# A two-layer attention backbone on one core: 622 further random shifts in the order of all queues

## The chip, the core and the metric

The kernel runs on one core of a Trainium2 chip. Its engines are TensorE (PE, matrix products), ScalarE (ACT), VectorE (DVE), GpSimd (POOL) and SyncE (SP, which here issues most of the DMAs). The metric is the time of one execution on the device in microseconds (us); several executions are run, and their median is given.

## What is computed

Two layers work on 512 latent tokens and 256 context tokens of width 1024. Each layer normalises and scales its input with factors that come from a conditioning vector, projects it, attends, gates, projects again, normalises and adds. Layer 0 uses differential attention (8 heads, each with two query and key halves of 64), layer 1 grouped-query attention (8 query heads, 2 key and value heads of 128, with normalised queries and keys). Cut to what matters:

```python
for i in range(2):
    shift, scale, gate = split3(silu(c) @ ada_w[i] + ada_b[i])     # and the same from c_ctx for the context
    h  = rms_norm(x, pre_g[i]) * (1 + scale) + shift
    q, k, v, z = split(h @ w_in[i])                                # context tokens alike
    q, k = rope(q), rope(k)                                        # latent tokens only
    if i == 0:                                                     # differential attention
        o = softmax(q1 k1^T / 8) v - lam * softmax(q2 k2^T / 8) v
        o = rms_norm(o, subln_g) * (1 - lam_init)
    else:                                                          # grouped-query attention
        o = softmax(rms(q) rms(k)^T / sqrt(128)) v
    x = x + gate * rms_norm((o * silu(z)) @ w_out[i], post_g[i])   # layer 0: the context stream too
```

Latent queries see latent and context keys in one softmax, context queries see only context keys.

## The kernel before

**Precision.** Every large product is made of three matmuls on operands split in a high and a low part (`mm3`): high by high, high by low, low by high. So each weight tile `raw` that a DMA brings is cast by ACT to `whi`, and POOL or DVE subtracts to get `wlo`; the activations `h` are split the same way, and so are the transposed softmax weights `at` (`ah` by ACT, `al` by DVE, in `split_at`).

**Stages.** First the conditioning factors of layer 0: groups of eight PE matmuls with 32 columns of output rows (`ag` tiles times `s`), ACT copies the result to `row`, PE spreads it with `sel`, DVE makes `mods`. In the same stretch PE transposes the normalised input (`xt` to PSUM, DVE and ACT copy it to `xnt`), and ACT scales it to `h`. Then layer 0: projections of query, key, value and gate, filled in between the attention of one head after the other. The attention of a head and block: PE makes scores into a double PSUM bank (`sc0`, `sc1`), DVE takes the maxima (`sm`), ACT the exponentials `pp` and `p`, DVE combines the two softmaxes in one product (`pp<-p,sm,pp`, SCALAR_TENSOR_TENSOR), transposes within 32 by 32 blocks (STREAM_TRANSPOSE), and SP moves the result to DRAM and back (`dr<-pp`, `at<-dr`) to complete the transposition; then the split, and PE multiplies by the values. Between heads, PE works through twelve groups of conditioning weights of 1 MB for what comes later (`grp_mm`, tile `araw`, one buffer, `grp_load`); ACT or DVE adds the result up in `arow`, DVE transposes it, PE folds it (`fold`), and DVE multiplies out the blocks that are wanted (`fo`, in `folded`). `sq<-bk,eps` is the logarithm by which ACT begins the normalisation of an attention output, out of the PSUM bank in which PE has made the sums of squares (`colsum`). Then the output projection of layer 0, `h` of layer 1 (`hf`, `h`), normalised keys (`kn`, scale `qrs`), and attention of layer 1 in the same way. PSUM has four single banks `bk0` to `bk3` and the two double ones, so that a group of matmuls often has to wait for the engine that empties its bank.

**What sets the order.** The program is run twice. First `Plan` records every instruction with what it reads and writes, works out who depends on whom, and prices each (`price`). Its list scheduler (`schedule`) then plays the program against these prices, picking on each engine the instruction that is ready first and, among those, the one with the lowest key. Twelve such passes (`PASSES`) give a key for each instruction. Then the tuple `MOVES` (line 102) is gone through: for each number in it, `shift` draws a random change of some keys, and a last play with the changed keys gives the order. The second run, `Emit`, issues the instructions, and `chain` ties each to the one before it on its engine, so that the order of the plan is the order on the chip. All instructions of the kernel therefore have one line in the profile, that of `Emit.add` (L526), and are told apart by their tiles.

```python
for s in MOVES:
    self.shift(random.Random(s), key, groups, side)
return self.schedule(lambda o: (key[o], o.n))
```

In `shift`, half of the numbers move a run of 1, 3, 8 or 20 PE groups (a group is all the matmuls into one PSUM output) by up to 30, 80, 200 or 500 in the key, together or each for itself; the other half move 1 to 40 neighbouring instructions of DVE, ACT, POOL or SP by up to 500, 1500 or 4000.

Of the kernel before, what the change touches and what calls it, by code (L numbers as in the profile page):

```python
# [94 lines left out]
def f32(ap):  # L95
# [40 lines left out]
    94403095, 584977676, 619944211, 22435410, 703825272, 621311326, 1059365364, 402415890, 143690719, 745221345,  # L136
    887241769, 694410056, 952138463, 289139968, 159032642, 434187675, 960054692, 918848355, 776950033, 866070713,
    362704586, 896208923, 1025137297, 255630178, 908876465, 71426820, 392273835, 223495391, 1023233858, 475503153,
    364577799, 282150972, 809075548, 442212720, 329900567, 892875344)
SLACK = 0  # L140


# [2255 lines left out]
```

## Time and profile before

| what | us |
|---|---|
| median of 3 runs | 742.43 |
| lowest and highest run | 741.39, 743.15 |
| the profiled execution | 742.12 |
| its span in the trace | 740.3 |
| PE busy | 724.4 |
| DVE, ACT, POOL busy | 545.5, 480.1, 458.6 |

The span runs from the first to the last instruction of the trace; 1.8 us of the profiled execution lie around it. A row of the timeline gives start and length in us, engine, line, operation, the tile written and the tiles read, shapes, and how many like instructions the row takes together; in brackets stands how long the engine was idle before it and what released it. A matmul's length in such a row includes its way through the array; the next one starts before it ends, so the pace of PE is read from start to start. PEld is the loading of weights into PE, which runs beside the matmuls.

### The profile page before, as it was taken

What the parts mean: (1) busy time and instruction counts of PE and PEld (TensorE: products, weight loads), DVE (VectorE), ACT (ScalarE), POOL (GpSimd) and SP (SyncE); (2) the same over time, 40 slices, a digit from 0 to 9 for tenths busy, and PEclk for the clock granted to TensorE, in tenths of its full rate; (3) what the DMA queues carried; (4) which work ended last, traced back from release to release, by engine and by line L of the source; (5) the groups of instructions that cost most, each with busy time, mean ns of one, the idle gap of its engine ahead of it and who ended that gap; (6) DMA issues with size and microseconds to landing.
All of it is one profiled execution on the core that took longest, in us unless ns stands there. A gap on an engine that the chain in (4) does not pass through costs nothing.

```text
span 740.3 us, 13930 instructions
## 1 busy us (share of the span) xinstructions
PE 724.4 (98%) x5008; PEld 648.5 (88%) x5008; DVE 545.5 (74%) x891; ACT 480.1 (65%) x1085; POOL 458.6 (62%) x506
## 2 busy tenths in 40 slices
PE   7999999999999999999999999999999999999996
PEld 6688888898888889888898998899999999988986
DVE  5555788769959876777798853699656789898844
ACT  6635467776577574766578943696366679679641
POOL 5363776785688775785855312447789959855201
PEclk9999999999999999999999999999999999999999
DMA  9941456454557575565557062453447678697613
GB/s 350 406 164 58 143 160 181 147 181 136 179 185 241 187 214 157 170 200 178 175 174 256 16 256 86 143 179 95 134 141 210 191 250 245 203 282 207 179 57 114
DMA packets 52596, 133.85 MB, mean 181 GB/s; under 512 B 6576, under 2 KB 27952, under 8 KB 50992
## 3 DMA queue, kind: packets, MB, share of 16 engines
q1 hardware_dynamic: 49104, 127.95, 54.1%
q10 hardware_dynamic: 3424, 5.02, 2.0%
q8 instruction: 39, 0.64, 0.4%
q14 instruction: 29, 0.24, 0.1%
HBM read 98.61 MB, written 30.15 MB: 174 GB/s over the span
## 4 chain that ended last, share of the span: by engine, by line
PE 68%; DVE 3%; POOL 2%; ACT 1%; issue 1%; DMA 1%; DVEq 0%; ACTq 0%
PE bk L526 56%; PE sc L526 11%; DMA araw<-in_ada_g 1%; POOL wlo L526 1%; POOL q L526 1%; DVE h L526 1%; DVE pp L526 1%; DVE hf L526 0%; ACT hf L526 0%; DVE sm L526 0%; POOL pp L526 0%; POOL qrs L526 0%; DVE sw L526 0%; ACT jk L526 0%; DVE gacc L526 0%
## 5 line engine op out<-in xcount | busy, mean ns | idle before, releaser
L526 PE MATMUL bk<-whi,h 128*128 128x256 f32 (+1 forms) x1184 | 247.3, 299 | 4.2 <-ACT sq L526 1.4
L526 PE MATMUL bk<-h,whi 128*128 128x512 f32 (+2 forms) x832 | 222.8, 348 | 0.0
L526 PEld LDWEIGHTS bk<-whi,h 128*128 128x128 f32 x1184 | 190.9, 188 | 14.8 <-ACT h L526 2.8
L526 POOL TENSOR_TENSOR wlo<-raw,whi 128x256 fp32r<-128x256 f32 x200 | 172.1, 885 | 46.2 <-ACT whi L526 45.7
L526 PE MATMUL bk<-wlo,h 128*128 128x256 f32 (+1 forms) x592 | 174.3, 297 | 0.0
L526 PEld LDWEIGHTS bk<-h,whi 128*128 128x128 f32 x832 | 145.2, 188 | 16.1 <-issue 3.4
L526 PE MATMUL bk<-h,wlo 128*128 128x512 f32 (+2 forms) x416 | 142.7, 348 | 0.0
L526 DVE TENSOR_REDUCE sm<-sc 128x1 f32<-128x768 f32 (+1 forms) x128 | 102.0, 814 | 23.8 <-PE sc L526 16.0
L526 PEld LDWEIGHTS bk<-wlo,h 128*128 128x128 f32 x592 | 110.9, 188 | 3.7
L526 POOL TENSOR_SCALAR pp<-pp,sm 128x768 f32<-128x768 f32 (+1 forms) x78 | 75.8, 976 | 51.0 <-DVE sm L526 34.8
L526 DVE TENSOR_TENSOR al<-at,ah 128x512 fp32r<-128x512 f32 x103 | 88.6, 877 | 16.5 <-ACT ah L526 11.8
L526 PEld LDWEIGHTS bk<-h,wlo 128*128 128x128 f32 x416 | 77.9, 188 | 6.5
L526 ACT CAST whi<-raw 128x1024 fp32r<-128x1024 f32 (+1 forms) x70 | 71.5, 1023 | 17.1 <-PE bk L526 10.9
L526 ACT CAST ah<-at 128x512 fp32r<-128x512 f32 x103 | 61.7, 620 | 14.6 <-PE bk L526 11.5
L526 DVE STREAM_TRANSPOSE pp<-pp 128x1536 f32<-128x1536 f32 (+1 forms) x39 | 61.4, 1575 | 3.0 <-POOL pp L526 2.9
L526 POOL TENSOR_TENSOR sz<-sz,za 128x384 f32<-128x384 f32 (+1 forms) x24 | 28.1, 1172 | 43.6 <-ACT za L526 43.6
L526 PEld LDWEIGHTS sc<-qk,qk 64*128 64x128 f32 x480 | 37.2, 185 | 15.3 <-ACT za L526 3.2
L526 ACT ACTIVATE jk<-bk 128x128 f32<-128x128 f32 (+4 forms) x66 | 22.8, 345 | 40.5 <-PE bk L526 21.3
L526 PE MATMUL sc<-qk,qk 64*128 64x256 f32 (+1 forms) x480 | 48.4, 337 | 0.0
L526 ACT ACTIVATE pp<-sc,sm 128x768 f32<-128x768 f32 (+1 forms) x46 | 35.5, 772 | 19.5 <-DVE sm L526 19.3
L526 DVE SCALAR_TENSOR_TENSOR pp<-p,sm,pp 128x768 f32<-128x768 f32 x32 | 43.8, 1368 | 3.7 <-POOL pp L526 2.9
L526 ACT ACTIVATE za<-za 128x384 f32<-128x384 f32 (+1 forms) x72 | 40.1, 562 | 7.6 <-DVE za L526 7.0
(218 smaller groups left out, 1356.2 us busy)
## 6 DMA issues: line engine op xcount, KB each, us to landing
dr<-pp SPq DMA_DIRECT2D x32, 768.0 KB, 4.0
at<-dr SPq DMA_DIRECT2D x128, 192.0 KB, 4.3
raw<-in_a_w SPq DMA_DIRECT2D x30, 512.0 KB, 4.2
araw<-in_ada_g SPq DMA_DIRECT2D x12, 1024.0 KB, 5.7
raw<-in_b_w SPq DMA_DIRECT2D x20, 512.0 KB, 3.6
ag<-in_ada_s SPq DMA_DIRECT2D x16, 512.0 KB, 9.0
raw<-in_w_out SPq DMA_DIRECT2D x16, 512.0 KB, 4.8
sw<-qr ACTq DMA_DIRECT2D x32, 128.0 KB, 3.2
```

The lines of the kernel that those rows point to most:

```text
L526: self.ops.append(getattr(eng, meth)(*args, **kw))
```

## The change

Only the tuple `MOVES` grows: it had 376 numbers, and 622 more are put behind the last, on 62 further lines. The first line that differs:

```diff
-    364577799, 282150972, 809075548, 442212720, 329900567, 892875344)
+    364577799, 282150972, 809075548, 442212720, 329900567, 892875344, 312439870, 458344974, 449572097, 562893025,
...
+    795406408, 794988788, 385261862, 383781077, 76324529)
```

The numbers were picked for orders that do well in plays of the program in which the landings of DMAs vary and some ACT, DVE and POOL instructions are lengthened at random. The planner, its prices, its passes and the program are the same, and so are the instructions and where their tiles lie: 4892 matmuls, 903 rows of ACT, 891 of DVE, 509 of POOL and 341 of SP in both. In the order, 3211 of the matmuls stand at another place (by up to 103 places), 391 rows of ACT (by up to 11), 372 of DVE (by up to 32), 211 of POOL and 126 of SP (by up to 4). The first 27 or so matmuls and PE's last 45 rows stay. The line of `Emit.add` is L588 after the change.

The prediction speaks of three places above all. In the rows below, a tile's name has its number and its place in the program behind it, and `x4` means four like rows in a run.

*The start, PE.* `ag` are the groups for the factors of layer 0, `xt_12` is a tile of input being transposed, `h_38` the first scaled input and `row_37`, `row_41` are copies of the groups' results. Before:

```order
L526 MATMUL sc1_75<-ident_76,xt_12_167 128x128
L526 MATMUL bk2_72<-sel4_138,row_37_276 128x2
L526 MATMUL sc1_75<-ident_76,xt_12_167 128x128
L526 MATMUL bk1_71<-ag_16_176,s32_134 32x256 x4
L526 MATMUL bk0_70<-whi_5_157,h_38_290 128x256
L526 MATMUL bk0_70<-wlo_6_158,h_38_290 128x256
L526 MATMUL sc0_74<-h_38_290,whi_1_153 128x512
```

After:

```order
L588 MATMUL sc1_75<-ident_76,xt_12_167 128x128 x8
L588 MATMUL bk0_70<-ag_14_171,s32_134 32x256 x4
L588 MATMUL bk1_71<-ag_16_176,s32_134 32x256 x4
L588 MATMUL bk2_72<-sel4_138,row_37_276 128x2 x2
L588 MATMUL bk1_71<-ag_17_178,s32_134 32x256 x4
L588 MATMUL bk0_70<-whi_5_157,h_38_290 128x256
L588 MATMUL bk0_70<-wlo_6_158,h_38_290 128x256
L588 MATMUL bk3_73<-sel4_138,row_41_302 128x2
```

`ag_14`, which stood ahead of all eight transposes of `xt_12`, now stands behind them; `ag_17`, which came twelve rows behind the first `h_38`, now stands ahead of it.

*ACT at the time of 174 us.* `pp_275` and `p_281` are the exponentials of one block of scores, `sq_233` is the logarithm that frees bank `bk0`. Before:

```order
L526 ACTIVATE pp_275_1973,sm_279_2062<-sc0_74,sm_282_2089 128x24x32
L526 ACTIVATE p_281_2088,sm_279_2062<-sc1_75,sm_283_2097 128x768
L526 ACTIVATE sq_233_1697<-bk0_70,eps_85 128x384
L526 ACTIVATE pp_273_1971,sm_279_2062<-sc0_74,sm_282_2089 128x8x32
L526 ACTIVATE at_274_1972,sm_279_2062<-sc1_75,sm_283_2097 128x256
L526 CAST vhi_270_1947<-bk1_71 128x256
```

After:

```order
L588 ACTIVATE pp_275_1973,sm_279_2062<-sc0_74,sm_282_2089 128x24x32
L588 ACTIVATE sq_233_1697<-bk0_70,eps_85 128x384
L588 ACTIVATE p_281_2088,sm_279_2062<-sc1_75,sm_283_2097 128x768
L588 ACTIVATE pp_273_1971,sm_279_2062<-sc0_74,sm_282_2089 128x8x32
L588 CAST vhi_270_1947<-bk1_71 128x256
L588 ACTIVATE at_274_1972,sm_279_2062<-sc1_75,sm_283_2097 128x256
```

`sq_233` has moved ahead of the second exponential.

*DVE at the time of 364 us.* `fo_591` empties bank `bk1` of a folded row, `pp_564` is a softmax block, `gT_470` an attention output, `al` are low parts of `at`. Before:

```order
L526 SCALAR_TENSOR_TENSOR gT_470_3525<-gT_470_3525,subg_112,sq_528_3911 128x768
L526 RECIPROCAL sm_572_4235<-sm_572_4235 128x2
L526 SCALAR_TENSOR_TENSOR za_584_4303<-sz_571_4210,za_584_4303 128x384
L526 TENSOR_SCALAR sm_572_4235<-sm_572_4235,nlam_122 128x2
L526 TENSOR_TENSOR vlo_590_4353<-bk2_72,vhi_589_4352 128x256
L526 TENSOR_TENSOR al_601_4538<-at_554_4097,ah_600_4537 128x512
L526 TENSOR_TENSOR fo_591_4368<-bk1_71,quad_149 128x32
L526 SCALAR_TENSOR_TENSOR pp_564_4172<-p_574_4261,sm_572_4235,pp_564_4172 128x24x32
```

After:

```order
L588 TENSOR_TENSOR al_601_4538<-at_554_4097,ah_600_4537 128x512
L588 TENSOR_SCALAR sm_572_4235<-sm_572_4235,nlam_122 128x2
L588 TENSOR_TENSOR al_603_4551<-at_554_4097,ah_602_4550 128x512
L588 TENSOR_TENSOR vlo_590_4353<-bk3_73,vhi_589_4352 128x256
L588 SCALAR_TENSOR_TENSOR za_584_4303<-sz_571_4210,za_584_4303 128x384
L588 SCALAR_TENSOR_TENSOR pp_564_4172<-p_574_4261,sm_572_4235,pp_564_4172 128x24x32
L588 TENSOR_TENSOR vlo_590_4353<-bk2_72,vhi_589_4352 128x256
L588 STREAM_TRANSPOSE pp_564_4172<-pp_564_4172 128x1536
L588 TENSOR_TENSOR fo_591_4368<-bk1_71,quad_149 128x32
```

`fo_591` has moved behind the product, the transpose, a further `al` and a further `vlo`; `gT_470`, which stood ahead of it, now comes two rows behind it.

61 rows, old and new, of the table MOVES are left out of this document.

## The prediction

> **What bounds the kernel now.** I read the page first, then TensorE's waits, then the timeline around each of those waits. The page's share of busy time:
>
> ```profile
> PE 724.4 (98%) x5008; PEld 648.5 (88%) x5008; DVE 545.5 (74%) x891; ACT 480.1 (65%) x1085; POOL 458.6 (62%) x506
> ```
>
> TensorE (PE) is busy for 98% of the span; the next engine, VectorE (DVE), for 74%. The change alters only orders, and the matmuls stay the same, so a gain can come only out of the time that PE stands still. The view of PE's waits lists all of that (total us, times, longest):
>
> ```profile
> PE bk L526 <- ACT sq L526: 1.4, 1, 1.4
> PE sc L526 <- DVE xt L526: 1.4, 1, 1.4
> PE bk L526 <- ACT h L526: 1.4, 2, 1.1
> PE sc L526 <- POOL xt L526: 1.3, 1, 1.3
> PE bk L526 <- DVE ones L526: 1.0, 1, 1.0
> PE bk L526 <- DMA araw<-in_ada_g: 0.8, 1, 0.8
> PE bk L526 <- DVE fo L526: 0.7, 1, 0.7
> PE bk L526 <- DVE kn L526: 0.6, 1, 0.6
> PE bk L526 <- ACT row L526: 0.5, 1, 0.5
> PE sc L526 <- DVE sm L526: 0.2, 1, 0.2
> PE bk L526 <- DVE h L526: 0.2, 1, 0.2
> ```
>
> They add to 9.5 us. The 1.0 behind `ones` is the first instruction of all and stays. So 8.5 us is the ceiling of any gain, 1.1% of the kernel; there is no such ceiling on a loss, since each of 4892 matmuls can begin to wait. PE's last 45 rows of the order are the same before and after, so the end of the kernel stays as it is. What PE pays for going from one kind of matmul to another I hold equal too: there are 34 runs of 64-row score matmuls in both orders, and 20 against 19 runs of 32-column ones.
>
> **The change part by part.** I followed each wait through the new order of its engines. The price of a matmul is needed throughout; PE's rows at one of the waits give it (start and length in us, then the operation, and in brackets the wait):
>
> ```profile
> 364.37 0.39 PE L526 MATMUL bk<-whi,h 128*128 128x256 f32 x1 [0.65 <-DVE fo L526]
> 364.59 0.28 PE L526 MATMUL bk<-wlo,h 128*128 128x256 f32 x1
> 364.71 0.40 PE L526 MATMUL bk<-whi,h 128*128 128x256 f32 x2
> ```
>
> With its inputs there, a matmul of 256 columns is followed by the next after 364.71 - 364.59 = 0.12, and so I put one of 384 columns at 0.18 (an estimate from the same two rows).
>
> *The start, to 25 us.* PE's rows around the first `h`, the scaled input of the projections:
>
> ```profile
> 15.32 0.85 PE L526 MATMUL sc<-ident,xt 128*128 128x128 f32 x6 [1.41 <-DVE xt L526]
> ...
> 18.44 0.38 PE L526 MATMUL bk<-whi,h 128*128 128x256 f32 x1 [1.13 <-ACT h L526]
> ...
> 20.75 0.64 PE L526 MATMUL bk<-ag,s 128*32 128x256 f32 x8
> 21.93 0.38 PE L526 MATMUL bk<-sel,row 128*128 128x2 f32 x2 [0.55 <-ACT row L526]
> ```
>
> Before, the group `ag_14` (eight matmuls of 256 columns, 0.64 like the row at 20.75) stands ahead of `xt_12` and runs while DVE still works on that; what is left of the wait is 1.41. After, it stands behind, and the transposes of `xt_12` can't start sooner than 15.32, since DVE is no sooner done. (Its load moves back by one place on SP, behind a weight tile's; that is hidden, as nobody asks for it before then.) So 0.64 moves out of idle time onto the path, and the first `h` reaches PE at about 18.44 + 0.6 = 19.05. Against that, `ag_17` (the row at 20.75) now stands ahead of that `h`, inside its 1.13 of idle time, and its `row` is copied long before PE asks for it, so that the 0.55 at 21.93 goes. From `h` to `ag_17` PE worked 20.75 - 18.44 = 2.31; the same work now ends at 19.05 + 2.31 = 21.36, and what stood behind the row at 21.93 goes on from there: 21.93 - 21.36, 0.6 sooner. Term: -0.6. Bounds: -1.2 (the 0.64 and the 0.55 both gained, if `h` isn't late) and +0.7 (the 0.64 lost, and a new wait for the second `h` in place of the rest).
>
> *`sq` at 174.* ACT's and PE's row. Behind them stand three that the next parts need: one softmax product `pp` on DVE with two POOL products running beside it, and one like it without:
>
> ```profile
> 172.58 0.89 ACT L526 ACTIVATE p<-sc,sm 128x768 f32<-128x768 f32 x1
> ```
> ```profile
> 174.09 0.39 PE L526 MATMUL bk<-whi,h 128*128 128x256 f32 x1 [1.41 <-ACT sq L526]
> ```
> ```profile
> 168.45 2.34 DVE L526 SCALAR_TENSOR_TENSOR pp<-p,sm,pp 128x768 f32<-128x768 f32 x1
> ```
> ```profile
> 222.78 1.01 DVE L526 SCALAR_TENSOR_TENSOR pp<-p,sm,pp 128x768 f32<-128x768 f32 x1
> ```
> ```profile
> 168.13 4.36 POOL L526 TENSOR_TENSOR qk<-qr,qk 128x768 fp32r<-128x768 f32 x2
> ```
>
> The logarithm `sq` reads PSUM bank bk0, and PE's next group wants that bank. It moves ahead of one exponential of 0.89, so the bank is free 0.89 sooner. Four matmuls fewer stand in front, which were 4 x 0.12 = 0.5 of cover. Term: 0.89 - 0.5, so -0.4; bounds 0 and -1.1 (with whatever ACT saves ahead of it).
>
> *`araw` at 263.5.* The load of one 1 MB weight tile, its wait, and a row of score matmuls for the price of one:
>
> ```profile
> 254.67 8.79 DMA araw<-in_ada_g
> ```
> ```profile
> 254.54 1.67 PE L526 MATMUL sc<-qk,qk 64*128 64x512 f32 x18
> ...
> 263.51 1.06 PE L526 MATMUL bk<-araw,s 128*32 128x512 f32 x8 [0.78 <-DMA araw<-in_ada_g]
> ```
>
> The tile has one buffer: its load starts when the group before has read it and must land before the next group. Between the two groups stood 27 matmuls of 384 columns and 13 of 256; now there are 34 and 15. That is 7 x 0.18 + 2 x 0.12 = 1.5 more cover, against 0.78 of waiting. Term: -0.8; bounds -0.8 and, if the load takes its longest under other traffic by the same 1.5, 0.
>
> *`fo` at 364.* DVE must take a folded row out of bank bk1 before PE's next group uses the bank; the wait, 0.65, is in the first of the three rows above. DVE's rows:
>
> ```profile
> 359.46 1.42 DVE L526 SCALAR_TENSOR_TENSOR gT<-gT,subg,sq 128x768 f32<-128x768 f32 x1
> ...
> 363.49 0.72 DVE L526 TENSOR_TENSOR al<-at,ah 128x512 fp32r<-128x512 f32 x1
> 364.14 0.18 DVE L526 TENSOR_TENSOR fo<-bk,quad 128x32 f32<-128x32 f32 x1
> 364.24 2.59 DVE L526 SCALAR_TENSOR_TENSOR pp<-p,sm,pp 128x768 f32<-128x768 f32 x1
> 366.76 0.41 DVE L526 TENSOR_TENSOR vlo<-bk,vhi 128x256 fp32r<-128x256 f32 x1
> 367.09 1.76 DVE L526 STREAM_TRANSPOSE pp<-pp 128x1536 f32<-128x1536 f32 x1
> ```
>
> On DVE, `fo` now comes behind the `pp` product, a `vlo`, the transpose and one more `al`, and ahead of `gT`: 2.59 + 0.41 + 1.76 + 0.72 - 1.42 = 4.06 later. On PE, 24 more matmuls of 256 columns and two fewer of 384 stand ahead of the fold (24 x 0.12 - 2 x 0.18 = 2.5), and between the fold and the waiting group there are 7 more of 384 and 12 score matmuls (7 x 0.18 + 12 x 1.67 / 18 = 2.4): 4.9 later in all. 4.06 less 4.9 takes 0.8 off a wait of 0.65: in time by 0.2, too little to be sure of. I take -0.5. Bounds: -0.65; and +0.9, if DVE is held up here by one more collision like that of the 2.34 row, against the lone 1.01 (1.33 late, less the 0.2 to spare, less some 0.2 that the other terms may leave PE behind).
>
> [...]
>
> *`kn` and `h` near 500.* Waits of 0.6 and 0.2 in the list above. DVE's rows up to `kn`, which empties a bank for PE:
>
> ```profile
> 498.27 0.75 DVE L526 SCALAR_TENSOR_TENSOR gacc<-gw,scol,gacc 128x512 f32<-128x512 f32 x1
> 498.94 0.69 DVE L526 TENSOR_TENSOR h<-hf,h 128x512 fp32r<-128x512 f32 x1
> 499.54 0.60 DVE L526 SCALAR_TENSOR_TENSOR kn<-bk,qrs,gq 128x128 f32<-128x128 f32 x2
> ```
>
> Two such subtractions `h` and two `gacc` steps now stand behind `kn` on DVE: up to 2 x 0.69 + 2 x 0.75 = 2.9 sooner. On PE, 12 matmuls of 256 columns and four short transposes (at no more than 0.12) ahead of the waiting group are gone: 16 x 0.12 = 1.9 sooner. That leaves 1.0 against 0.6, if `kn`'s other input, a scale from ACT, comes as early. I take -0.4, with bounds of -0.6 and +0.4 (`kn` won no more than 1.5). For `h`, one of two halves of the step before it now stands behind it: -0.2, bounds -0.2 and 0.
>
> *All the rest.* 3211 matmuls change place, by up to 103 places, and 126 of SP's 341 rows, by up to 4; no other wait is there to be removed. What I could not follow can only add waits. The six terms make -0.6 - 0.4 - 0.8 - 0.5 - 0.4 - 0.2 = -2.9; I give back a quarter of this, 0.7, for new small ones: the list above holds four waits of 0.2 to 0.6, so two such. Sum: -2.2 on the profiled execution (742.12 with a span of 740.3, so 1.8 around it, unchanged). The median of the runs is 742.43, 0.3 above the profiled one; from the median, 742.4 - 2.2 = 740.2.
>
> **The rivals.** 0.2% is 1.5 us, about what a measurement can tell from no change: faster is below 740.95, slower above 743.9.
>
> *Nothing moves.* The waits re-form elsewhere. For it: the terms of `fo` and `kn` win by putting other work of DVE behind (`gT`, two `h`, two `gacc`), and `h` is itself a line in the list of waits. Against it: that list holds nothing of `gT` or `gacc`, so these had some room. If the give-back is the whole 2.9 instead of 0.7: 742.4.
>
> *Slower, by collisions.* The product `pp` starts a chain: transpose, round trip through DRAM, split, matmul. A collision costs 2.34 - 1.01 = 1.33 us on it. If the new order makes four more that PE has no lead left to hide, 4 x 1.33 = 5.3 against the 2.9 won: 742.4 + 2.4 = 744.8. It decides from the third on (4.0 - 2.9 = +1.1), and slower as I call it from the fourth. For it: 32 of these products run, and nothing in an order keeps them off POOL's. Against it: before, the collisions at 168 and 364 cost PE nothing that its list of waits shows under `pp` or `at`.
>
> **How the numbers follow.** The forecast case has 0.60; its own range is 742.4 - 4.5 = 737.9 (every term at its better bound, with nothing given back) to 741.0. Nothing moves: 0.22, between 741.0 and 743.9. Slower: 0.18, of which 0.14 for the collisions and 0.04 for the upper bounds of the start and `fo` coming together (+0.7 + 0.9 with the other terms at naught). The range for 8 in 10 leaves out a tail of the forecast case below 737.8 and most of the slower case: 737.8 to 744.0. Likeliest: 740.2.
>
> **What would show it.** In PE's waits after: no `araw`, no or a smaller `fo`, `kn` and `row`, `sq` at 1.0 or less, and the first `h` about 0.6 later but the second earlier; the sum of waits at about 7.3. I am wrong if the sum of PE's waits is as before or higher, if waits for `at`, `ah` or `al` appear that were not there, or if the waits fall and the span does not, which would say that matmuls themselves issue more slowly in the new order.

## The result and the profile after

Six executions of each kernel, in turns on one chip: 738.1 us after (737.15 to 739.76) against 742.14 before (741.39 to 743.15), 4.0 us less; the ratio is 0.9948, with a 95% interval of 0.9934 to 0.9961. The forecast was 740.2, between 737.8 and 744.0. So the direction and the range held, the latter by 0.3, and the gain was almost twice the forecast. The profiled execution took 738.26, with a span of 736.5 against 740.3.

The page's share of busy time, and the whole list of PE's waits, of the changed kernel:

```profile
PE 723.0 (98%) x5008; PEld 647.4 (88%) x5008; DVE 555.1 (75%) x891; ACT 478.0 (65%) x1085; POOL 460.7 (63%) x506
```
```profile
PE sc L588 <- POOL xt L588: 2.7, 1, 2.7
PE sc L588 <- DVE xt L588: 1.6, 1, 1.6
PE bk L588 <- DVE ones L588: 1.0, 1, 1.0
PE bk L588 <- ACT h L588: 0.9, 2, 0.7
PE bk L588 <- POOL q L588: 0.4, 1, 0.4
PE sc L588 <- DVE sm L588: 0.2, 1, 0.2
```

The waits add to 6.8 instead of 9.5. Gone are `sq`, `araw`, `fo`, `kn`, `row` and the `h` near 496. New is `q` behind POOL, and the first wait, for `xt`, has grown from 1.3 to 2.7. That makes 2.7 less, while the span fell by 3.8, so the list does not hold everything. A second way to read the trace does: for each matmul take the time to the start of the next, take off what is usual for its shape (the median over both executions), and add up what is left along the program. The table has this sum by stretch, placed by equal work of PE; times are those of the kernel before.

| stretch, us | left over before | after | difference | term of the prediction |
|---|---|---|---|---|
| start to 28 | 8.4 | 9.0 | +0.6 | -0.6 |
| 28 to 141 | 2.5 | 2.3 | -0.2 | |
| 141 to 184 (`sq`) | 3.1 | 1.4 | -1.7 | -0.4 |
| 184 to 245 | 1.0 | 1.0 | +0.1 | |
| 245 to 266 (`araw`) | 1.3 | 0.2 | -1.1 | -0.8 |
| 266 to 348 | 1.7 | 1.9 | +0.2 | |
| 348 to 369 (`fo`) | 1.1 | 0.2 | -0.9 | -0.5 |
| 369 to 491 | 2.1 | 2.1 | 0.0 | |
| 491 to 533 (`kn`, `h`) | 2.0 | 0.5 | -1.5 | -0.6 |
| 533 to 635 | 1.6 | 1.5 | -0.1 | |
| 635 to 655 (`q`) | 0.1 | 0.7 | +0.6 | |
| 655 to 715 | 0.0 | 0.1 | +0.2 | |

The levels depend on what is taken as usual, so only the differences are read. They make -3.8, the whole of what the span lost. The difference sits where the prediction looked for it, at four places, and at two places the new order lost 0.6 each. Three sizes were well off: the start, `sq`, and the stretch behind 491.

**The start.** PE's rows in the changed kernel, and three stretches of 2 us (bounds, length, busy us of PE, PEld, DVE, ACT, POOL, then the granted clock of TensorE, the DMA share and GB/s):

```profile
12.22 1.08 PE L588 MATMUL bk<-ag,s 128*32 128x256 f32 x8
13.24 1.52 PE L588 MATMUL sc<-ident,xt 128*128 128x128 f32 x8
16.36 1.07 PE L588 MATMUL sc<-ident,xt 128*128 128x128 f32 x8 [1.60 <-DVE xt L588]
17.36 1.07 PE L588 MATMUL bk<-ag,s 128*32 128x256 f32 x16
```
```profile
10.00:12.00 2.00, 1.77 (x11) 1.43 (x9) 1.86 (x4) 1.49 (x4) 0.55 (x1) 0.69 1.04 409
12.00:14.00 2.00, 2.00 (x14) 0.97 (x13) 0.75 (x2) 1.19 (x3) 1.28 (x2) 0.50 1.05 418
14.00:16.00 2.00, 0.76 (x6) 0.52 (x4) 1.14 (x2) 0.57 (x2) 1.41 (x2) 0.96 1.00 399
```

TensorE's granted clock fell to 0.50 between 10 and 12 us (0.69 in the mean there) and was back by about 14: the group at 12.22 took 1.08, where the group of the same shape before the change took 0.64. The transposes of `xt_12` begin at 16.36, a full 1.0 later than before. So this start had a second cause of lateness, which the prediction did not know of.

This fall does not come from the move of `ag_14`: that group's old place is at 13.28, behind the fall, and up to there PE's order is the old one. What differs ahead of it is PE's first wait for `xt`, 2.7 against 1.3. The only other of the fourteen profiles with a fall as early (the kernel before with `ag_14` late, below) has a first wait of 2.4, the other twelve have 1.2 to 2.2. That the long wait brings the fall fits this, but no run tests it.

**The place at 174.** VectorE's product, POOL's two products beside it, and the logarithm:

```profile
168.36 1.00 DVE L588 SCALAR_TENSOR_TENSOR pp<-p,sm,pp 128x768 f32<-128x768 f32 x1
169.29 1.81 DVE L588 TENSOR_REDUCE sm<-sc 128x1 f32<-128x768 f32 x2
```
```profile
168.67 2.41 POOL L588 TENSOR_TENSOR qk<-qr,qk 128x768 fp32r<-128x768 f32 x1
```
```profile
171.16 0.58 ACT L588 ACTIVATE sq<-bk,eps 128x384 f32<-128x384 f32 x1
```

Before, the product began at 168.45, 0.32 behind POOL's (168.13), and took 2.34. Now it begins at 168.36, 0.31 ahead of POOL's (168.67), and takes 1.00; what took longer is POOL's, 2.41. The maxima, the exponentials and the logarithm all hang on it: the logarithm starts 2.3 sooner (171.16 against 173.46), of which only 0.89 is its new place in ACT's queue.

### The profile page after: what moved, and what is told of

The parts are those of the page before. It is cut to its first block, busy times and chain, and to the rows that moved or that the text cites. A ratio compares the mean times of both kernels' runs of the same rounds, so it can differ in the third digit from the quotient of the medians.

```text
span 736.5 us, 13920 instructions
## 1 busy us (share of the span) xinstructions
PE 723.0 (98%) x5008; PEld 647.4 (88%) x5008; DVE 555.1 (75%) x891; ACT 478.0 (65%) x1085; POOL 460.7 (63%) x506
## 4 chain that ended last, share of the span: by engine, by line
PE 91%; POOL 3%; DVE 2%; issue 2%; ACT 1%; DVEq 0%; POOLq 0%; ACTq 0%
PE bk L588 74%; PE sc L588 17%; POOL wlo L588 1%; POOL q L588 1%; POOL pp L588 0%; DVE hf L588 0%; ACT hf L588 0%; POOL qrs L588 0%; ACT h L588 0%; ACT jk L588 0%; DVE h L588 0%; DVE gacc L588 0%; DVE xt L588 0%; POOL xt L588 0%; POOL sm L588 0%
## 5 line engine op out<-in xcount | busy, mean ns | idle before, releaser
L588 PE MATMUL bk<-whi,h 128*128 128x256 f32 (+1 forms) x1184 | 245.5, 299 | 1.1 <-ACT h L588 0.9
L588 PE MATMUL bk<-h,whi 128*128 128x512 f32 (+2 forms) x832 | 224.9, 348 | 0.0
L588 PEld LDWEIGHTS bk<-whi,h 128*128 128x128 f32 x1184 | 190.5, 188 | 12.8 <-ACT h L588 2.3
L588 POOL TENSOR_TENSOR wlo<-raw,whi 128x256 fp32r<-128x256 f32 x200 | 167.4, 862 | 42.2 <-ACT whi L588 35.7
L588 PE MATMUL bk<-wlo,h 128*128 128x256 f32 (+1 forms) x592 | 170.6, 297 | 0.0
L588 PEld LDWEIGHTS bk<-h,whi 128*128 128x128 f32 x832 | 145.5, 188 | 15.5 <-issue 2.5
L588 PE MATMUL bk<-h,wlo 128*128 128x512 f32 (+2 forms) x416 | 143.6, 348 | 0.0
L588 DVE TENSOR_REDUCE sm<-sc 128x1 f32<-128x768 f32 (+1 forms) x128 | 101.8, 814 | 28.3 <-PE sc L588 19.2
L588 PEld LDWEIGHTS bk<-wlo,h 128*128 128x128 f32 x592 | 109.7, 188 | 3.6 <-DVE wlo L588 0.3
L588 POOL TENSOR_SCALAR pp<-pp,sm 128x768 f32<-128x768 f32 (+1 forms) x78 | 78.4, 1009 | 51.2 <-DVE sm L588 44.9
L588 DVE TENSOR_TENSOR al<-at,ah 128x512 fp32r<-128x512 f32 x103 | 96.6, 957 | 14.6 <-ACT ah L588 8.5
L588 PEld LDWEIGHTS bk<-h,wlo 128*128 128x128 f32 x416 | 78.2, 188 | 7.8 <-issue 0.8
L588 ACT CAST whi<-raw 128x1024 fp32r<-128x1024 f32 (+1 forms) x70 | 71.4, 1024 | 19.5 <-PE bk L588 8.7
L588 ACT CAST ah<-at 128x512 fp32r<-128x512 f32 x103 | 61.7, 620 | 17.5 <-PE bk L588 15.5
L588 DVE STREAM_TRANSPOSE pp<-pp 128x1536 f32<-128x1536 f32 (+1 forms) x39 | 61.4, 1575 | 1.7 <-POOL pp L588 1.6
L588 POOL TENSOR_TENSOR sz<-sz,za 128x384 f32<-128x384 f32 (+1 forms) x24 | 31.1, 1298 | 46.4 <-ACT za L588 40.6
L588 PEld LDWEIGHTS sc<-qk,qk 64*128 64x128 f32 x480 | 37.3, 185 | 15.2 <-issue 3.4
L588 ACT ACTIVATE jk<-bk 128x128 f32<-128x128 f32 (+4 forms) x66 | 22.8, 346 | 40.1 <-PE bk L588 22.3
L588 PE MATMUL sc<-qk,qk 64*128 64x256 f32 (+1 forms) x480 | 48.4, 337 | 0.0
L588 ACT ACTIVATE pp<-sc,sm 128x768 f32<-128x768 f32 (+1 forms) x46 | 35.6, 774 | 18.8 <-DVE sm L588 18.7
L588 ACT ACTIVATE za<-za 128x384 f32<-128x384 f32 (+1 forms) x72 | 40.5, 565 | 6.9 <-DVE za L588 6.2
L588 DVE SCALAR_TENSOR_TENSOR pp<-p,sm,pp 128x768 f32<-128x768 f32 x32 | 40.7, 1273 | 3.0 <-POOL pp L588 2.0
```

Source lines behind the costliest of these rows:

```text
L588: self.ops.append(getattr(eng, meth)(*args, **kw))
```

## The experiments

Two helpers edit the order between the plan and the issue. `put(order, n, m)` takes the recorded instruction number n out and sets it directly ahead of number m (with True: behind it); every other row stays in its place. `splice` takes one order up to a planned time and from there all that is left in the other order; 376 numbers of `MOVES` are the old order and 998 the new one. Nothing else differs from the kernel before or the changed kernel. These runs were made on three chips, on which the kernel before has medians of 740.74, 740.9 and 740.98; each run is compared with the kernel before on its own chip. The ratio and its interval come from all executions compared, and not from the two medians.

### The logarithm alone

The kernel before, with `sq` ahead of the exponential `p`:

```diff
-        em.chain(pl.plan())
+        order = pl.plan()
+        put(order, 1535, 1696)
+        em.chain(order)
```

> The kernel before with one ACT row moved: the logarithm that frees bank bk0 at 174 us stands ahead of the second exponential. Theory Q (the prediction's term: what PE waits for at 174 is the place of the logarithm in ACT's queue): PE's wait of 1.41 there falls by the exponential's 0.89 to about 0.5; time -0.9. Theory C (in the changed kernel most of the 1.6 us won there came from VectorE's product pp at 168.4, which took 1.00 instead of 2.34 because it began before POOL's product and not after it): here the product still takes 2.3, the wait falls to 0.5 as well, and not to nothing as in the changed kernel.

Measured: 740.51 against 740.9, ratio 0.9995 (0.9986 to 1.0003), so the time alone does not tell it from no change. PE's waits at this place:

```profile
PE bk L532 <- ACT sq L532: 0.5, 1, 0.5
PE sc L532 <- ACT at L532: 0.4, 1, 0.4
```
```profile
167.94 2.34 DVE L532 SCALAR_TENSOR_TENSOR pp<-p,sm,pp 128x768 f32<-128x768 f32 x1
```

The wait for `sq` fell from 1.41 to 0.52, by the 0.89 that both theories gave. But the exponentials behind it came later, and PE waits 0.4 for the last of them instead, at the next scores. The balance of the place is -0.44. VectorE's product still took 2.34. So ACT's order is worth what the prediction gave for it, by another sum, and is a quarter of what the changed kernel won here.

### Two casts exchanged, and exchanged back

The changed kernel differs at this place in two more ACT rows, the casts that POOL's products wait for. The kernel before with them in the new order, `put(order, 1717, 1715)`:

> The kernel before with two neighbouring ACT casts at 167 us exchanged, so that the cast for POOL's first qk product comes second, as in the changed kernel. Theory C: POOL's product starts about 0.5 us later, after VectorE's pp product has begun; that product takes 1.0 instead of 2.34, everything behind it comes 1.3 sooner, and PE's wait for the logarithm falls from 1.41 to about 0.1; time -1.3. Theory Q: the casts have nothing to do with it, the wait stays at 1.4 and the time at 742.

The changed kernel with them in the old order, `put(order, 1715, 1717)`:

> The changed kernel with the same two casts put back in their old order, all else new. Theory C: the product pp meets POOL's again and takes about 2.3; the logarithm ends 1.3 later, and PE, which needs the bank about 0.8 after it came free, waits about 0.5 again; time +0.5. Theory Q: no change.

Measured: 740.82 (ratio 0.9999, 0.999 to 1.0008) for the first and 737.62 (0.9952, 0.9937 to 0.9967, against the kernel before) for the second. VectorE's and POOL's product in the first, then in the second:

```profile
167.86 2.51 DVE L532 SCALAR_TENSOR_TENSOR pp<-p,sm,pp 128x768 f32<-128x768 f32 x1
```
```profile
167.71 4.36 POOL L532 TENSOR_TENSOR qk<-qr,qk 128x768 fp32r<-128x768 f32 x2
```
```profile
166.81 1.03 DVE L594 SCALAR_TENSOR_TENSOR pp<-p,sm,pp 128x768 f32<-128x768 f32 x1
```
```profile
166.98 2.57 POOL L594 TENSOR_TENSOR qk<-qr,qk 128x768 fp32r<-128x768 f32 x1
```

My guess at what delays POOL was wrong: the casts moved POOL's start by about 0.17 in the first and by as little in the second, too little to change who begins first. Which of the two begins first is still what the durations follow, 0.15 behind: 2.51, 0.17 ahead: 1.03.

### The product ahead of POOL's

The direct trial: in the kernel before, the product goes ahead of the block transpose that stood before it on VectorE, `put(order, 1592, 1479)`.

> The kernel before with one VectorE row moved at 167 us: the product pp stands ahead of the transpose (1.76) that came before it, so that it begins ahead of POOL's first qk product. Theory C (the collision): pp takes about 1.0 instead of 2.34, the maxima behind it and with them the exponentials come 1.3 sooner, PE's wait of 1.41 for the logarithm at 174 falls to 0.1; time -1 (the transpose, 1.0 later, must not be missed by PE). Theory Q (only the place in ACT's queue counts): pp still takes 2.3 somewhere and the wait stays at 1.4.

Measured: 739.57 against 740.74, ratio 0.9983 (0.9974 to 0.9992), 1.2 us faster by one row.

```profile
166.30 1.02 DVE L532 SCALAR_TENSOR_TENSOR pp<-p,sm,pp 128x768 f32<-128x768 f32 x1
```
```profile
PE sc L532 <- ACT pp L532: 0.4, 1, 0.4
PE bk L532 <- ACT sq L532: 0.2, 1, 0.2
```

The product took 1.02 and the wait for `sq` fell from 1.41 to 0.2; the balance of the place is -1.15. The new wait of 0.4 stands at 389 us, far behind it. With the -0.44 of the logarithm alone this makes -1.6, against -1.7 in the changed kernel. So 1.2 of the place is the collision and 0.4 the order of ACT, if the two add up; no run has just these two together. Part of the price goes to POOL: the product now begins 0.22 ahead of another of its rows (`sqs` at 166.52), which takes 1.68 instead of 1.02, and PE does not wait for that one. All fourteen profiles agree: in the six with the old order here and VectorE's row in its place, the product begins 0.15 to 0.32 behind POOL's and takes 2.34 to 2.51; in the other eight (the new order, and this kernel) it begins ahead and takes 0.99 to 1.03. What in the new order brings VectorE those 0.63 us forward against POOL can be read in part. Measured from VectorE's transpose ahead of the product, POOL's row ahead of its own (`sqs`) begins at +0.40 before (167.15 against 166.75) and at +0.86 after (167.52 against 166.66), which is 0.46; the other 0.16 or so is the casts. Why `sqs` comes later is not settled.

### The later `fo` without PE's work in front

The kernel before with `fo` behind the transpose, as in the changed kernel, `put(order, 3658, 3583, True)`:

> The kernel before with one VectorE row moved at 364 us: fo stands behind the product pp, the vlo and the transpose, as in the changed kernel, but PE's order is the old one. If PE's 4.9 us of work put ahead are what hides the later fo (the prediction's term), PE waits here for 0.65 + 2.59 + 0.41 + 1.76 = 5.4 us, and the time rises by 4.8, less what later waits give back. If fo was not what PE waited for, it rises by less than 1.

Measured: 748.18 against 740.74, ratio 1.0098 (1.0085 to 1.0112). PE's row, and PE's clock in the stretches around it:

```profile
367.46 0.58 PE L532 MATMUL bk<-whi,h 128*128 128x256 f32 x1 [5.21 <-DVE fo L532]
```
```profile
362.00:366.00 4.00, 0.25 (x2) 0.00 (x0) 4.00 (x5) 0.62 (x1) 3.51 (x3) 1.00 0.05 17
366.00:370.00 4.00, 2.54 (x12) 2.54 (x13) 1.80 (x3) 0.00 (x0) 0.62 (x2) 0.50 0.47 197
```

The wait is 5.2, near the 5.4 expected. The loss is 7.4, more than the 4.8 expected: from 366 us, within the wait, the granted clock is 0.50, PE's matmuls of 256 columns follow each other behind it after 0.21 us instead of 0.12, and a wait of 1.8 for an exponential comes at 397. So `fo` alone is a bad move, and PE's matmuls put in front are what makes it harmless. The moves come in pairs, and one engine's half may not be judged by itself.

### The start by itself, and the kernel without it

The new order up to 30 us, then the old one; and the reverse:

```diff
-        em.chain(pl.plan())
+        order = splice(pl.plan, (998, 30), (376, 1000000000.0))
+        em.chain(order)
```

> The new order up to the planned time of 30 us on all engines, the old order behind it. The prediction's term for the start is -0.6. Theory S (the start of the new order is a gain, and the profiled execution of the changed kernel lost 0.6 there only because TensorE's granted clock was at 0.5 to 0.7 from 10 to 14 us in it): with a clock near 1.0 in the start the second h reaches PE at about 24.2 and the median falls by 0.6. Theory L (the later ag_14 group and the later landings make the start itself slower): the median rises by 0.3 to 0.6, also where the clock is near 1.0.

> The old order up to the planned time of 30 us on all engines, the new order behind it. Theory S2 (after the first round of runs: the new start wins about 0.4 where TensorE keeps its clock, but leaves TensorE so little busy between 12 and 17 us that in a third to a half of its executions the granted clock falls to 0.5 for some 4 us, which costs 2 to 4 us; the rest of the new order wins about 4): no execution has a mean clock below 0.996, the runs scatter within 1 us but for single ones, and the median lies 0.5 to 1 below that of the changed kernel, which is 4 to 4.5 below the kernel before. Theory N (the dips of the clock come by chance in any order): the scatter is that of the changed kernel, a third of the runs at a clock of 0.996 or less.

The new start alone: 741.76 against 740.9, ratio 1.0014 (0.9998 to 1.0031). Its twelve executions fall in two kinds: eight at a mean clock of 0.997 to 0.999, from 740.03 to 741.97, and four at 0.991 or 0.992, from 744.2 to 745.93. The kernel before lay, in 28 of 29 executions, between 740.43 and 742.06 at 0.997 or more. The upper kind is not free of dips: its profiled execution, 741.83 at a mean of 0.997, has one (0.80 from 14 to 16 us, 0.50 from 16 to 18, 0.85 from 18 to 20), so that a count of means up to 0.996 leaves out short ones. So both theories had a part of it: undisturbed, the start is worth about -0.4 (740.03 against 740.43 for the fastest; the three executions at 0.999 have a median of 740.43, nine of the kernel before at 0.999 one of 740.89), near the -0.6 of the prediction. With the dips the median is 0.9 higher, in an interval that just includes no change. Theory S was wrong to take the dip for chance.

The old start with the new rest: 738.57 against 740.74, ratio 0.9971 (0.996 to 0.9982). Five of six executions were at 0.998 or 0.999, so the dips were rare, but the median did not come down as expected. PE's list of waits has two that the changed kernel's has not:

```profile
PE sc L597 <- ACT pp L597: 1.0, 1, 1.0
PE bk L597 <- ACT ah L597: 0.4, 1, 0.4
```

They stand at 662 us (`ah`) and 667 us (`pp`), some 30 us behind the wait for `q` at 635, and add to 1.4. The wait for `q` is next.

### POOL's row at 636

POOL's rows up to `q` in the changed kernel, and PE's wait for it:

```profile
632.99 0.69 POOL L588 TENSOR_TENSOR qrs<-qrs,mhalf 128x2 f32<-128x2 f32 x1
633.67 0.92 POOL L588 TENSOR_SCALAR pp<-pp,sm 128x768 f32<-128x768 f32 x1
634.54 1.25 POOL L588 TENSOR_TENSOR q<-ta,tb 128x256 f32<-128x256 f32 x1
```
```profile
635.85 0.33 PE L588 MATMUL bk<-ident,q 128*128 128x128 f32 x1 [0.44 <-POOL q L588]
```

The changed kernel with one subtraction of POOL's set behind `q`, `put(order, 6561, 6550, True)`:

> The changed kernel with one POOL row moved: the product q, for which PE waits at 636 us, goes ahead of one subtraction wlo of 0.73 that stood six rows before it. If POOL's queue sets that wait (POOL runs there without a gap from 619 to 636, while PE has come 4.6 sooner and POOL's q only 3.4), the wait of 0.44 goes and the stretch from 630 to 640 wins back the 0.6 that it lost: time -0.5. If q waits for its inputs from VectorE, nothing changes.

Measured: 738.19 against 740.74, ratio 0.9967 (0.9952 to 0.9982), with executions from 736.13 to 742.61, five of twelve of them at a clock of 0.996 or less. In the profile the wait is gone and the stretch from 633 to 655 us costs nothing:

```profile
631.95 0.91 POOL L594 TENSOR_SCALAR pp<-pp,sm 128x768 f32<-128x768 f32 x1 [0.41 <-ACT sm L594]
632.83 0.74 POOL L594 TENSOR_TENSOR q<-ta,tb 128x256 f32<-128x256 f32 x1
```

POOL now has a pause of 0.41 ahead of `q`, so its queue had set the wait. The time by itself can't show 0.5 here, since the scatter that the start brings is ten times that.

### What in the start lets the clock fall

Four kernels side by side. The changed kernel itself:

> The changed kernel itself, beside the others on one chip. If the dips of TensorE's clock belong to its start (theory D), a third to a half of its executions have a mean clock of 0.996 or less and lie 1 to 5 us above the rest; the rest lie at about 737.0, 3.7 below the kernel before. If the kernel has nothing of the kind (theory N), all lie within 1 us and at 0.997 to 0.999, as the kernel before does.

The old start, the new rest, and POOL's row:

> The old order up to 30 us, the new one behind it, and POOL's subtraction wlo moved behind the product q at 636 us. Theory D and the POOL theory together: no dips of the clock, and neither the q wait nor what came of it from 640 to 660 us when the start was old (2.0 us); the median is 4.5 to 5.2 below the kernel before, near 735.8, within 1 us. If the 2.0 us at 640 to 660 have another cause than the late q, about 738 remains.

The changed kernel with POOL's row, and with `ag_14` and its load put back:

```diff
+        put(order, 121, 107)
+        put(order, 122, 107)
+        put(order, 123, 107)
+        put(order, 124, 107)
+        put(order, 49, 54)
+        put(order, 6561, 6550, True)
```

> The changed kernel with q ahead of the subtraction, and with one part of its start undone: the group ag_14 ahead of the transposes of xt_12 again, and its load ahead of the weight tile's. Theory D1 (what lets the clock fall is that TensorE has too little to do from 12 to 16 us, since this group went from there): the dips go, the median is near 736. Theory D2 (another part of the start does it): a third of the executions at 0.996 or less, as in the changed kernel, and the median near 738.

The kernel before with `ag_14` set behind `xt_12`, and the two `row_37` matmuls behind `ag_16`:

> The kernel before with that one part of the new start: on PE the group ag_14 behind the transposes of xt_12, and the two row_37 matmuls, which need it, behind ag_16. Theory D1: a third of the executions show a mean clock of 0.996 or less and lie 2 to 4 us above the rest. Theory D2: no more of them than in the kernel before. In both, the 0.64 of the group moves onto the path and the other executions lie 0.5 to 1 above the kernel before, as ag_17 stays where it was.

| kernel | median | ratio to before (95%) | executions, us | at a clock of 0.996 or less |
|---|---|---|---|---|
| before | 740.98 | 1 | 740.65 to 743.46 | 1 of 16 |
| changed | 739.62 | 0.9972 (0.9957 to 0.9986) | 736.93 to 741.89 | 5 of 11 |
| old start, POOL's row | 737.91 | 0.9955 (0.9943 to 0.9967) | 736.79 to 738.83 | 0 of 5 |
| `ag_14` early, POOL's row | 736.32 | 0.9933 (0.992 to 0.9946) | 735.65 to 737.24 | 0 of 5 |
| before, `ag_14` late | 745.06 | 1.006 (1.0042 to 1.0077) | 743.53 to 747.87 | 5 of 6 |

(One execution of the first two rows each, far out, is left out of the last two columns.) One group of four rows in PE's order switches the dips on in the old order, and in the new one they are gone with it back in its place: theory D1. The first half is clear (5 of 6 against 3 of 115 with the group early). The second rests on five executions, where a share of 17 in 45, that of the new start, would give none about once in ten times; each edit also moves a little more (a load, or the two `row_37` matmuls). The profile of the last row has a fall at 10.7 like that of the result's, and a second one from 17.6 on, behind the group's new place. That row also rose by more than was expected without a dip: its execution at 0.997 is 2.7 above the kernel before, not 0.5 to 1. A short dip may hide in it, so that the price of the group itself is not measured there.

The third row missed its expectation of 735.8. In its profile the waits for `pp` and `ah` are gone together with that for `q`, so in these two profiles they go with the late `q`, but the median came down by only 0.7 from the old start's 738.57, which was measured on another chip. The stretches around it, of the changed kernel here (with a dip) and of the one with `ag_14` early:

```profile
12.00:14.00 2.00, 0.97 (x8) 0.73 (x8) 1.29 (x4) 1.32 (x4) 1.73 (x3) 1.00 1.04 424
14.00:16.00 2.00, 1.06 (x8) 0.86 (x8) 0.79 (x1) 1.33 (x2) 1.98 (x3) 0.94 1.00 404
16.00:18.00 2.00, 2.00 (x18) 0.69 (x17) 0.69 (x1) 0.80 (x2) 2.00 (x4) 0.50 1.05 418
```
```profile
12.00:14.00 2.00, 1.79 (x20) 1.01 (x16) 1.29 (x4) 1.39 (x3) 1.46 (x3) 1.00 1.03 422
14.00:16.00 2.00, 0.80 (x8) 0.83 (x8) 1.05 (x2) 1.81 (x3) 1.98 (x3) 1.00 1.03 416
```

From 12 to 14 us PE is busy for 0.97 with `ag_14` late and for 1.79 with it early; the clock falls behind the first and stays at 1.00 behind the second. PE's one long wait there, for `xt`, is 2.0 in the first and 1.4 in the second. It does not bring a dip each time: four profiles with the new start have the same wait of 1.97; in two of them (here, and the new start alone) the clock falls, in the other two (the casts back, and POOL's row) it stays at 1.00. PE was not idle throughout ahead of the fall: it was busy for half of the 4 us from 12 to 16. The falls differ in length. If the clock is either 1.00 or 0.50, 2 us with a mean m hold 4 x (1 - m) us at 0.50; that makes an estimated 3.4 us in the profile of the new start alone (means of 0.80, 0.50 and 0.85) and in that of the result (0.69, 0.50 and 0.96), while the fall here holds 0.50 in each stretch from 16 to 22 us. How little work it takes for a fall, and why only some executions show one, is not shown by these runs.

The last but one row of the table beats both kernels: 736.32, 3.3 below the changed one beside it. Its start has no dips, and behind the start only one wait is left in PE's list, 0.8 for a `sq`. Its first group of 512 columns:

```profile
21.30 1.06 PE L594 MATMUL bk<-ag,s 128*32 128x512 f32 x8
```

In the profile of the kernel before, the same group begins at 22.25, and in the changed kernel's, with its clock at 0.50 from 12 to 14 us, at 22.89. So the term of -0.6 for the start is there to be had, and more, with `ag_14` early: there the clock held, with 0 of 5 executions at 0.996 or less.

## Why the prediction was right, and where it was not

The forecast rested on one reading, that PE's pace is fixed and its waits are all there is to win, and on four places where the order takes a wait away. The second held: the difference of the span is in those places. The first failed in the start, where the granted clock fell to 0.50 and the group at 12.22 took 1.08 instead of 0.64. The result was -4.0 against -2.2. In the later measurement beside the other kernels of the last experiment it gained less, 1.4 between the medians at a ratio of 0.9972, with deeper dips of the clock (means down to 0.990, where the result's six reach 0.995), so that how far the size was off depends on the dips too. The steps:

- **All waits, by 0.26 each.** The list counts a wait from the modelled end of the matmul before. At 174 PE's rows before the change are these (the second stands in the prediction too):

```profile
172.40 0.28 PE L526 MATMUL bk<-wlo,h 128*128 128x256 f32 x1
174.09 0.39 PE L526 MATMUL bk<-whi,h 128*128 128x256 f32 x1 [1.41 <-ACT sq L526]
174.31 0.28 PE L526 MATMUL bk<-wlo,h 128*128 128x256 f32 x1
```

  Without a wait the second would have begun at 172.40 + 0.12 and the third 0.12 later, so 1.67 goes with a wait listed as 1.41. With 0.26 more on each, the waits for `araw`, `fo`, `kn` and `h` that went (0.78, 0.65, 0.56, 0.18) come to 1.04, 0.91, 0.82 and 0.44, against 1.1, 0.9 and 1.5 (the last two together) in the table. So the 8.5 was not the ceiling that I called it.
- **The start, -0.6.** Half right. That `ag_14` costs 0.64 on the path and `ag_17` wins more in the idle time held where the clock holds (about -0.4): there the first `h` comes at 18.75 and 18.92 (the casts back, POOL's row), 0.3 to 0.5 later than before, near the 0.6 of the prediction; in the result's profile it comes at 20.32. The step that failed treated the start as a matter of waits alone. Moving `ag_14` took 0.8 us of work out of the stretch from 12 to 14 us, and 17 of the 45 executions with this start and a known clock have a mean clock of 0.996 or less, against 3 of 115 with `ag_14` early (leaving out the kernel with the late `fo`, which has a dip of its own). In the median of the run with the new start alone the term was +0.9, not -0.6. The result's own profile lost its 0.6 to a dip that came ahead of `ag_14`'s place, whose cause stays open.
- **`sq` at 174, -0.4.** The term named was right (-0.44 alone), but it was not what the place was worth: -1.7. The rows for the rest stood in the prediction, the 2.34 of the product at 168.45 and POOL's at 168.13, and served as the price of the slower rival. The step that failed was to ask only whether new collisions would come, and not whether this one, which began with a margin of 0.32 and ended in the longest wait of the list, would go.
- **`araw`, -0.8.** The number came out, but not for the reason given. Of the seven profiles with the old order at this place, one more showed the wait (1.0) and five none, in kernels that differ from the one before by rows elsewhere; of the seven with the new order three showed it (0.6, 0.3, 0.2) and four did not. Its mean is (0.78 + 1.0) / 7 = 0.25 in the old order and 1.1 / 7 = 0.16 in the new one. The 7 + 2 matmuls of cover changed nothing that can be seen in seven profiles each; the wait looks like the chance of one landing, and the term should have been near zero. Besides, three of the seven with the new order have a wait of 0.45 to 0.8 for a logarithm `sq` at 265 to 269, just behind, which none with the old order has; the changed kernel's profile happens to be one without it. So on this stretch the profile was lucky.
- **`fo`, -0.5.** The wait went, and the pair of moves works as described: without PE's half the wait is 5.2 (5.4 by the rows). The size was off by the 0.26 above, and because the wait went whole, with room to spare: `fo` ended at 363.92, and the group that needs its bank begins at 366.53, behind twelve score matmuls from 365.29 on. That is 2.6 to spare, where the prediction had 0.2 (DVE's rows of the changed kernel here and at the next place, then PE's):

```profile
363.78 0.14 DVE L588 TENSOR_TENSOR fo<-bk,quad 128x32 f32<-128x32 f32 x1
...
493.75 0.61 DVE L588 SCALAR_TENSOR_TENSOR kn<-bk,qrs,gq 128x128 f32<-128x128 f32 x2 [1.21 <-ACT qrs L588]
```
```profile
365.29 1.31 PE L588 MATMUL sc<-qk,qk 64*128 64x512 f32 x12
```

- **`kn` and `h`, -0.6.** -1.5 in the balance. Both waits went, as described: `kn` ends at 494.36, and the next row of PE's beside it shows no wait. The rest is time that the list of waits does not show: the 0.26 twice, and, before, short transposes for `gacc` that began 0.2 late (at 502.06, for one) where a wait was too short to count.
- **The give-back, +0.7.** It was +0.6 behind the start, at one place, `q`; the size is luck in part, as the wait at 265 missed this profile. It is neither of the rivals in full: PE drew ahead by 4.6 us and POOL, which had no pause of note from 619 to 636, only by 3.4, so that POOL became what PE waited for.

The slower rival, collisions, was the right mechanism with the wrong sign. It is worth 1.2 us at the one place where it was measured, in favour of the new order.

## What to carry to other kernels

A wait list prices what goes, but each wait has a chain behind it: follow it back to the first row that is longer than its like, and ask of a new order whether that row becomes shorter, before asking what else may become longer. A wait for a DMA that stands once in one profile is not a term until a second profile shows it. And count TensorE's busy time after the change in a stretch where it has little to do, as matmuls may not be free to leave it: here, with 0.8 us less of it from 12 to 14 us, 17 of 45 executions had a mean clock of 0.996 or less, against 3 of 115.

## What the runs showed of the hardware

- Of VectorE's product `pp` and POOL's product `qk` at the place of `sq` (`sqs` in the kernel with the product put ahead), the one that began first kept its short time and the other took longer, in each of the fourteen profiles: VectorE's took 0.99 to 1.03 when 0.17 to 0.34 us ahead, and 2.34 to 2.51 when 0.15 to 0.32 behind, while `qk` took 2.41 and 2.57 when behind (the result, and the casts back), and 1.84 when ahead (in the kernel before with `ag_14` late, whose two rows stand below). The 1.01 at 222.78, which the prediction calls lone, had POOL's subtractions `wlo` beside it, at 222.20 and 222.90: the second, 0.12 behind the product, took 1.50, where one at 217.32 took 0.74.

```profile
174.80 1.84 POOL L532 TENSOR_TENSOR qk<-qr,qk 128x768 fp32r<-128x768 f32 x1
```
```profile
175.12 2.34 DVE L532 SCALAR_TENSOR_TENSOR pp<-p,sm,pp 128x768 f32<-128x768 f32 x1
```

- The granted clock fell to 0.50 in a wait of 5.2 us in the middle of the kernel too (the late `fo`), and stayed there until about 372.9 (its mean from 370 to 374 is 0.64): an estimated 2.5 us on top of the wait, as the 25 matmuls of 256 columns from 367.46 to 372.92 took 5.46, where 25 x 0.12 make 3.0. In the start it fell beside a wait of 1.97 in two of four profiles, in one of them with PE busy for 0.97 and 1.06 in two stretches of 2 us.
- The same program scattered by 5 us between executions (736.93 to 741.89), the fastest at a mean clock of 0.999 and the slowest at 0.990, where the kernel before scattered by 1.4 in 15 of 16.
